# Weight read-backs issued by GpSimd instead of SyncE

## The chip, the core and the metric

One core of a Trainium2 chip runs the whole program. The metric is the time of one execution on the device in microseconds (us), as the median of several runs. The engines are named as the profile names them: PE (TensorE matmuls), PEld (TensorE weight loads), DVE (VectorE), ACT (ScalarE), POOL (GpSimd), SP (SyncE, which here does nothing but issue DMAs; SPq is its queue).

## What is computed

One layer of an encoder is applied to two inputs, a prompt of 1024 rows ("p") and a sample of 512 rows ("s"), with the same weights and a model width of 2048. All data are 32-bit floats.

```
h    = rmsnorm(x, pre_g)
proj = h @ w_in                       # 2048 x 5984, kept as 47 strips of 128 columns
q, k, v, gates, c_q, c_kv, k_pe, z    = parts of proj
o_a  = gated delta rule over q, k, v  # 8 heads, two directions, chunked scan
o_b  = softmax attention from c_q, c_kv (w_uq, w_uk, w_uv) and a rotary key, 8 heads
mix  = [o_a * silu(z_a), o_b * silu(z_b)]
y    = x + rmsnorm(mix @ w_out, post_g)
```

## The kernel before

Every large product is done in three passes. A weight tile is split into a high part `whi` and a rest `wlo`, each of 128 x 512 floats (256 KB), and the operand likewise into `hi` and `lo`; PE adds hi*whi, lo*whi and hi*wlo. `whi` and `wlo` together are called a piece here. A piece serves four k-tiles of 128.

The prompt goes through the input projection first (0 to about 1070 us). There a piece is loaded raw, ACT makes `whi` and POOL makes `wlo` (`split`, L199), and both are stored to DRAM (`spill`, L231). Later stages read the stored parts back instead of splitting again. There are two places that do so, L220 and L254:

- `kept_piece` (L220) for the input projection of the sample, 47 strips of 4 pieces of 2 reads, 376 reads, about 1070 to 1870 us. Beside it PE runs the delta rule (the `gdn_` functions).
- `read_back` (L254) for `mla_prep` (12 pieces for each of 3 blocks of 512 rows, 72 reads, about 1870 to 2070 us), for `attention` (32 reads), and for the first block of the output projection (`out_proj` with `more` set: 64 pieces, 128 reads, from about 2500 to 2867 us).

That makes 608 reads of 256 KB. A read waits until PE has finished with the buffer that it fills; there are four buffers of `whi` and of `wlo` in the projections and in `mla_prep` (`self.wb`, `read_back(..., 4)`), so up to three pieces can be on their way or ready ahead of the one in use.

All DMAs of the program are issued by SP, in one queue and in order: x and weight loads, read-backs, stores of results between the stages, the loads of the delta rule (`KQ`, `vp`, `ktok`, `dd`, `lam`, `lt`) and the swaps of `rope` (L567, L568). PE's order is written out by the program's own planner (`merge`, with a running time `self.t`); the order on the other engines is set by a scheduler from its own estimate of when each instruction can start.

POOL's work in the stages with read-backs: the running sum of squares of the sample (L313, 15 additions), clearing of two columns of `cin` (L349, L350), clearing of diagonal blocks (L776, which waits for the `dU` store), sums of squares (L381, L393), the sine product of `rope` (L570, which waits for the four or two swap DMAs), the softmax factors in `attention` (L1085, 160 times), and in the output projection the gain (L1219) and, from the second block on, the splits of `w_out` (L199).

Inside `out_proj` the first block is cut in parts: columns f = 0, 1, 2 over the first eight pieces, f = 3 over all sixteen, then f = 0, 1, 2 over the last eight. At the end of each of these last three, POOL runs L1219 four times.

Of the kernel before, what the change touches and what calls it, by code (L numbers as in the profile page):

```python
# [7 lines left out]
F32 = mybir.dt.float32  # L8
# [49 lines left out]
class Kern:  # L58
# [153 lines left out]
    def kept_piece(self, q, f, kt, lo_eng):  # L212

        nc, S = self.nc, self.scratch
        names = [f"w{v}{f}.{kt}" for v in "hl"]
        if q == "s":
            w = []
            for name, tag in zip(names, ("whi", "wlo")):
                t = self.wp.tile([P, 4, P], F32R, tag=tag, name=tag, bufs=self.wb)
                nc.sync.dma_start(t.bitcast(F32), S[name])  # L220
                w.append(t)
            return w
        return self.spill(names, self.a["w_in"][f][:, kt:kt + 4, :], lo_eng)
# [25 lines left out]
    def read_back(self, name, p, sfx, bufs):  # L249

        w = []
        for v, tag in zip("hl", ("whi", "wlo")):
            t = p.tile([P, 4, P], F32R, tag=tag + sfx, name=tag, bufs=bufs)
            self.nc.sync.dma_start(t.bitcast(F32), self.scratch[name + v])  # L254
            w.append(t)
        return w

# [1189 lines left out]
```

## Time and profile before

| | us |
|---|---|
| median of 3 runs | 3249.65 (3247.64 to 3258.47) |
| profiled execution, its own time | 3257.81 |
| its span in the trace | 3256.0 |
| PE busy | 3130.6 |
| DVE busy | 1643.3 |
| POOL busy | 885.1 |

The profiled execution's own time is 1.8 us more than the span that its trace covers. Busy times are sums over the span; issuing a DMA does not count as busy. The trace's granted clock of PE is 0.94 to 1.00 of full speed in every stage. Times within the span are counted from its start.

### The profile page before, as it was taken

What the parts mean: (1) busy time and instruction counts of PE and PEld (TensorE: products, weight loads), DVE (VectorE), ACT (ScalarE), POOL (GpSimd) and SP (SyncE); (2) the same over time, 40 slices, a digit from 0 to 9 for tenths busy, and PEclk for the clock granted to TensorE, in tenths of its full rate; (3) what the DMA queues carried; (4) which work ended last, traced back from release to release, by engine and by line L of the source; (5) the groups of instructions that cost most, each with busy time, mean ns of one, the idle gap of its engine ahead of it and who ended that gap; (6) DMA issues with size and microseconds to landing.
All of it is one profiled execution on the core that took longest, in us unless ns stands there. A gap on an engine that the chain in (4) does not pass through costs nothing.

```text
span 3256.0 us, 47971 instructions
## 1 busy us (share of the span) xinstructions
PE 3130.6 (96%) x16554; PEld 2611.5 (80%) x16554; DVE 1643.3 (50%) x4000; ACT 1159.2 (36%) x2736; POOL 885.1 (27%) x806
## 2 busy tenths in 40 slices
PE   7999999999999899999999988899999999899998
PEld 6788888888888788888888877688788878777876
DVE  7233443444410536765665477688887555240213
ACT  4223333333321313333333232465666444232231
POOL 5434434444432300000000011122222212044452
PEclk9999999999999999999999999999999999999999
DMA  6777777777776765566655697433223353764454
GB/s 242 248 229 236 241 242 242 240 233 244 242 244 203 256 197 181 182 193 198 212 177 179 215 302 250 151 97 90 67 89 119 101 188 117 247 217 126 149 175 133
DMA packets 405620, 626.10 MB, mean 192 GB/s; under 512 B 90544, under 2 KB 141736, under 8 KB 403840
## 3 DMA queue, kind: packets, MB, share of 16 engines
q1 hardware_dynamic: 405376, 623.04, 59.8%
q8 instruction: 130, 2.13, 0.3%
q14 instruction: 114, 0.93, 0.1%
HBM read 388.44 MB, written 230.90 MB: 190 GB/s over the span
## 4 chain that ended last, share of the span: by engine, by line
PE 74%; DMA 10%; DVE 8%; issue 3%; ACT 2%; POOL 2%; SPq 2%; DVEq 0%; POOLq 0%; ACTq 0%
PE mm L272 15%; PE mm L276 15%; PE mm L273 15%; PE py L1205 3%; PE py L1204 3%; PE py L1206 3%; DMA wraw<-w_out 2%; PE pt L1124 2%; PE Tp L841 2%; POOL wlo L199 1%; DVE UA L736 1%; PE py L904 1%; PE pu L923 1%; PE po L1102 1%; PE po L1101 1%
## 5 line engine op out<-in xcount | busy, mean ns | idle before, releaser
L272 PE MATMUL mm<-hi,whi 128*128 128x512 f32 x2256 | 899.6, 402 | 14.4 <-ACT whi L196 8.4
L273 PE MATMUL mm<-lo,whi 128*128 128x512 f32 x2256 | 877.4, 391 | 6.5 <-DVE lo L305 6.3
L199 POOL TENSOR_TENSOR wlo<-wraw,whi 128x512 fp32r<-128x512 f32 x400 | 561.2, 1412 | 750.5 <-ACT whi L196 610.6
L276 PE MATMUL mm<-hi,wlo 128*128 128x512 f32 x2256 | 763.8, 391 | 0.0
L196 ACT ACTIVATE whi<-wraw 128x512 fp32r<-128x512 f32 x400 | 248.6, 630 | 863.2 <-PE mm L273 314.1
L272 PEld LDWEIGHTS mm<-hi,whi 128*128 128x128 f32 x2256 | 425.6, 189 | 99.4 <-ACT whi L196 9.1
L273 PEld LDWEIGHTS mm<-lo,whi 128*128 128x128 f32 x2256 | 425.3, 189 | 90.9 <-DVE lo L305 9.4
L276 PEld LDWEIGHTS mm<-hi,wlo 128*128 128x128 f32 x2256 | 424.6, 188 | 91.0 <-DMA wlo<-wl43.4_8663 0.2
L1204 PE MATMUL py<-whi,mhi 128*128 128x512 f32 x768 | 303.4, 395 | 10.8 <-DVE y L1219 6.9
L1205 PE MATMUL py<-wlo,mhi 128*128 128x512 f32 x768 | 303.8, 396 | 6.8 <-POOL wlo L199 6.4
L1206 PE MATMUL py<-whi,mlo 128*128 128x512 f32 x768 | 302.4, 394 | 0.0
L1085 POOL TENSOR_TENSOR pe<-pe,af 128x512 f32<-128x512 f32 x160 | 166.2, 1056 | 491.1 <-DVE af L1083 202.7
L356 DVE SCALAR_TENSOR_TENSOR acc<-cin,conv_w,acc 128x1024 f32<-128x1024 f32 (+1 forms) x192 | 209.7, 1092 | 36.4 <-ACT acc L354 31.8
L352 DVE TENSOR_TENSOR cin<-mm,rbh 128x512 f32<-128x512 f32 x72 | 47.4, 687 | 302.5 <-PE mm L276 263.1
L1204 PEld LDWEIGHTS py<-whi,mhi 128*128 128x128 f32 x768 | 144.8, 189 | 45.9 <-DVE y L1219 8.0
L1205 PEld LDWEIGHTS py<-wlo,mhi 128*128 128x128 f32 x768 | 144.8, 189 | 43.7 <-POOL wlo L199 11.5
L1206 PEld LDWEIGHTS py<-whi,mlo 128*128 128x128 f32 x768 | 144.8, 189 | 31.9
L1071 ACT ACTIVATE pe<-s,am 128x512 f32<-128x512 f32 x160 | 110.3, 690 | 107.2 <-DVE am L1070 98.6
L1219 DVE TENSOR_TENSOR y<-py,g 128x512 f32<-128x512 f32 x36 | 24.7, 690 | 239.0 <-ACT junk L1218 235.5
L360 DVE TENSOR_TENSOR acc<-mm,rbh 128x512 f32<-128x512 f32 x48 | 31.7, 687 | 223.7 <-PE mm L276 212.5
L199 DVE TENSOR_TENSOR ptl<-pt,pth 128x512 fp32r<-128x512 f32 x160 | 109.8, 686 | 46.8 <-ACT pth L196 45.9
L1070 DVE TENSOR_REDUCE am<-s 128x1 f32<-128x512 f32 x160 | 109.5, 685 | 35.2 <-PE s L1067 34.6
(449 smaller groups left out, 5035.2 us busy)
## 6 DMA issues: line engine op xcount, KB each, us to landing
wraw<-w_out SPq DMA_DIRECT2D x192, 256.0 KB
wraw<-w_in SPq DMA_DIRECT2D x188, 256.0 KB
dd<-dX SPq DMA_DIRECT2D x48, 256.0 KB
x<-xT_p SPq DMA_DIRECT2D x16, 512.0 KB
xres<-x_p SPq DMA_DIRECT2D x8, 1024.0 KB
y_p<-y SPq DMA_DIRECT2D x32, 256.0 KB
x<-xT_s SPq DMA_DIRECT2D x16, 256.0 KB
xres<-x_s SPq DMA_DIRECT2D x4, 1024.0 KB
```

What stands on the lines that cost most here:

```text
L196: nc.scalar.activation(hi, src, AF.Copy)
L199: (lo_eng or nc.vector).tensor_sub(lo, src, hi.bitcast(F32))
L272: nc.tensor.matmul(ps, whi[:, k], hi[:, s], start=kt == 0, stop=False)
L273: nc.tensor.matmul(ps, whi[:, k], lo[:, s], start=False, stop=False)
L276: nc.tensor.matmul(ps, wlo[:, k], hi[:, s], start=False, stop=kt == KT - 1)
L356: nc.vector.scalar_tensor_tensor(acc, cin[:, j:j + T], w[:, f, j:j + 1], acc, op0=ALU.mult, op1=ALU.add)
L1070: nc.vector.tensor_reduce(m[:, k:k + 1], o, axis=AX.X, op=ALU.min)
L1071: nc.scalar.activation(pe[k], o, AF.Exp, bias=m[:, k:k + 1], scale=-1.0, accum_out=l[:, k:k + 1])
L1085: nc.gpsimd.tensor_mul(pe[k2], pe[k2], f[:, k2:k2 + 1].to_broadcast([P, BLK]))
L1204: nc.tensor.matmul(ps, hi[:, c], w[0], start=kt == kts[0], stop=False)
L1205: nc.tensor.matmul(ps, hi[:, c], w[1], start=False, stop=False)
L1206: nc.tensor.matmul(ps, lo[:, c], w[0], start=False, stop=kt == kts[1] - 1)
```

## The change

Both read-backs are issued by GpSimd. Nothing else is edited.

```diff
             for name, tag in zip(names, ("whi", "wlo")):
                 t = self.wp.tile([P, 4, P], F32R, tag=tag, name=tag, bufs=self.wb)
-                nc.sync.dma_start(t.bitcast(F32), S[name])
+                nc.gpsimd.dma_start(t.bitcast(F32), S[name])
                 w.append(t)
...
             t = p.tile([P, 4, P], F32R, tag=tag + sfx, name=tag, bufs=bufs)
-            self.nc.sync.dma_start(t.bitcast(F32), self.scratch[name + v])
+            self.nc.gpsimd.dma_start(t.bitcast(F32), self.scratch[name + v])
             w.append(t)
```

The scheduler places the reads among POOL's other instructions, so that SP's queue loses 608 entries and POOL's gains them. PE's order is the same but for a few rows in the attention stage. Three places follow, each with POOL's rows before and now. `wh33.4` is the high part of strip 33 from k-tile 4 on, `uq4h` the high part of strip 4 of w_uq, `o11.1l` the rest of k-tile 11 and column block 1 of w_out.

POOL at the start of the sample's input projection, before:

```order
L313 TENSOR_TENSOR rbh<-rbh,x 128x512
L637 MEMSET dd_9081 128x512
L313 TENSOR_TENSOR rbh<-rbh,x 128x512 x12
L349 MEMSET cin 128x2
L350 MEMSET cin 128x2
L313 TENSOR_TENSOR rbh<-rbh,x 128x512 x2
```

And now, around the last additions:

```order
L313 TENSOR_TENSOR rbh<-rbh,x 128x512 x5
L220 DMA whi<-wh33.0_746 128x512
L220 DMA wlo<-wl33.0_748 128x512
L220 DMA whi<-wh33.4_780 128x512
L220 DMA wlo<-wl33.4_782 128x512
L349 MEMSET cin 128x2
L350 MEMSET cin 128x2
L313 TENSOR_TENSOR rbh<-rbh,x 128x512 x3
```

The last three additions stand behind four reads.

POOL in `mla_prep`, before:

```order
L776 MEMSET UA 32x16x32 x4
L570 TENSOR_TENSOR rxs<-rxs,sin 128x512
L570 TENSOR_TENSOR rxs<-rxs,sin 64x512
L570 TENSOR_TENSOR rxs<-rxs,sin 128x512 x4
L570 TENSOR_TENSOR rxs<-rxs,sin 64x512
L570 TENSOR_TENSOR rxs<-rxs,sin 128x512 x2
```

And now:

```order
L776 MEMSET UA 32x16x32 x3
L254 DMA whi<-uq2h 128x512
L254 DMA wlo<-uq2l 128x512
L570 TENSOR_TENSOR rxs<-rxs,sin 128x512
L254 DMA whi<-uq3h 128x512
L254 DMA wlo<-uq3l 128x512
L254 DMA whi<-uq10h 128x512
L254 DMA wlo<-uq10l 128x512
L570 TENSOR_TENSOR rxs<-rxs,sin 64x512
L254 DMA whi<-uq4h 128x512
L254 DMA wlo<-uq4l 128x512
L254 DMA whi<-uq5h 128x512
```

Two to six reads stand between one sine product and the next.

POOL in the second half of the output projection's first block, before:

```order
L1219 TENSOR_TENSOR y_26029<-y_26029,g 128x512
L1219 TENSOR_TENSOR y_26030<-y_26030,g 128x512
L1219 TENSOR_TENSOR y_26031<-y_26031,g 128x512
L1219 TENSOR_TENSOR y_26032<-y_26032,g 128x512
L1219 TENSOR_TENSOR y_26029<-y_26029,g 128x512
```

And now, at the change from column block 0 to column block 1:

```order
L254 DMA wlo<-o10.1l 128x512
L254 DMA whi<-o10.1h 128x512
L1219 TENSOR_TENSOR y_26029<-y_26029,g 128x512
L254 DMA wlo<-o11.1l 128x512
L254 DMA whi<-o11.1h 128x512
L1219 TENSOR_TENSOR y_26030<-y_26030,g 128x512
L1219 TENSOR_TENSOR y_26031<-y_26031,g 128x512
L1219 TENSOR_TENSOR y_26032<-y_26032,g 128x512
L254 DMA wlo<-o12.1l 128x512
L254 DMA whi<-o12.1h 128x512
```

The reads of pieces 11 and 12 of the new column block stand behind gain products of the old one.

## Rows read from the trace of the kernel before

**Rows 1.** The page: busy time and share by engine; then the chain.

```profile
PE 3130.6 (96%) x16554; PEld 2611.5 (80%) x16554; DVE 1643.3 (50%) x4000; ACT 1159.2 (36%) x2736; POOL 885.1 (27%) x806
...
PE 74%; DMA 10%; DVE 8%; issue 3%; ACT 2%; POOL 2%; SPq 2%; DVEq 0%; POOLq 0%; ACTq 0%
```

**Rows 2.** Stretches by stage: start to end, length, busy us and instructions by engine.

```profile
core 0: us, PE busy (x) PEld busy (x) DVE busy (x) ACT busy (x) POOL busy (x), PEclk, DMA share, GB/s
1070.00:1122.00 52.00, 42.89 (x183) 33.54 (x181) 28.48 (x55) 18.82 (x39) 23.04 (x24) 0.94 0.90 318
1122.00:1870.00 748.00, 742.17 (x4320) 626.77 (x4321) 437.78 (x1418) 240.89 (x711) 30.15 (x83) 0.99 0.61 192
1870.00:2070.00 200.00, 175.03 (x1038) 144.09 (x1037) 141.03 (x382) 61.28 (x191) 28.29 (x23) 0.99 0.83 267
...
2500.00:2780.00 280.00, 266.58 (x1496) 224.98 (x1495) 153.00 (x333) 126.67 (x293) 63.60 (x61) 0.99 0.47 150
2780.00:2890.00 110.00, 100.98 (x431) 81.27 (x430) 40.48 (x61) 34.12 (x70) 25.45 (x19) 0.97 0.70 228
```

**Rows 3.** Waits of SP's queue, whole span: us in total, times, longest.

```profile
SPq L220 <- PE mm L276: 357.1, 152, 8.7
...
SPq L254 <- PE py L1206: 66.2, 36, 5.7
...
SPq L254 <- PE pq L610: 14.5, 8, 6.5
```

**Rows 4.** Line 254: one read's issue on SP (ns, min/median/max), and who waited.

```profile
L254 SPq DMA_DIRECT2D whi<-uq8h x3: 383/433/435, 1872.3 to 1983.4; - x3
...
  PE pq L608: 3.5, 1
  PE kp L1014: 2.2, 1
```

**Rows 5.** Waits of PE, 1870 to 2070 us.

```profile
PE kk L731 <- DVE z L969: 4.6, 1, 4.6
PE pk L882 <- DVE oacc L938: 4.6, 6, 1.2
PE py L904 <- DVE oacc L894: 4.4, 4, 1.9
```

**Rows 6.** Waits of DVE in the same stretch.

```profile
DVE rx L569 <- DMA rxs<-rx: 9.6, 4, 3.7
```

**Rows 7.** POOL groups, 1870 to 2070 and 2780 to 2890: busy, mean ns | idle before.

```profile
L570 POOL TENSOR_TENSOR rxs<-rxs,sin 128x512 f32<-128x512 f32 (+1 forms) x15 | 24.1, 1610 | 151.9 <-DMA rxs<-rx 112.6 <-DMA rxs<-kpe 24.1 <-DVE clo L591 10.0
...
L1219 POOL TENSOR_TENSOR y<-y,g 128x512 f32<-128x512 f32 x12 | 16.6, 1405 | 90.7 <-ACT junk L1218 90.7
```

**Rows 8.** The page's groups: the softmax factors on POOL.

```profile
L1085 POOL TENSOR_TENSOR pe<-pe,af 128x512 f32<-128x512 f32 x160 | 166.2, 1056 | 491.1 <-DVE af L1083 202.7
```

**Rows 9.** Waits of PE, 1070 to 1122, then 2070 to 2780 us.

```profile
PE xcols L325 <- POOL rbh L313: 0.7, 1, 0.7
...
PE pt L1124 <- POOL pe L1085: 1.4, 3, 1.0
```

**Rows 10.** PE in time, 2786 to 2787 us: two products three matmuls apart.

```profile
2786.25 0.39 PE L1206 MATMUL py<-whi,mlo 128*128 128x512 f32 x1
...
2786.93 0.39 PE L1206 MATMUL py<-whi,mlo 128*128 128x512 f32 x1
```

**Rows 11.** POOL in time, 1870 to 2070 us: start, length, [idle before it].

```profile
1894.54 1.29 POOL L570 TENSOR_TENSOR rxs<-rxs,sin 128x512 f32<-128x512 f32 x1 [20.22 <-DMA rxs<-rx]
...
1956.22 1.79 POOL L570 TENSOR_TENSOR rxs<-rxs,sin 128x512 f32<-128x512 f32 x1 [18.59 <-DMA rxs<-rx]
...
2016.08 1.29 POOL L570 TENSOR_TENSOR rxs<-rxs,sin 128x512 f32<-128x512 f32 x1 [15.38 <-DMA rxs<-rx]
```

**Rows 12.** Tile pq, 1870 to 2070 us: ns min/median/max, first and last start.

```profile
L608 PE MATMUL pq<-chi,whi x144: 389/398/988, 1875.3 to 2056.0; 128*128 128x512 f32 x144
```

**Rows 13.** The chain, 1910 to 1920 us: a read's time from issue to landing.

```profile
1912.76 5.53 DMA whi<-uq11h
```

## The prediction

> **What bounds the kernel now.** I read the page's busy line and chain first. PE is busy 3130.6 of 3256.0 us, and 74% of the chain that ended last is PE [rows 1]. All that any change off PE can win is therefore in PE's idle time, 125 us, and the stages with read-backs hold only part of that. The table of stretches says which part [rows 2]: the start of the sample's projection has 9.1 us of idle PE (52.0 - 42.9), its long body 5.8 (748.0 - 742.2), `mla_prep` 25.0 (200.0 - 175.0), the attention from 2500 on 13.4, the rest of the first output block 9.0.
>
> The reads do hold up SP's queue: SP stood 357.1 us before a read of line 220 and 66.2 + 14.5 us before one of line 254, always until PE had freed a buffer [rows 3]. All that is behind such a read in the queue waits with it. But almost nobody waits for the reads: the two largest waits for a read of line 254 are 3.5 and 2.2 us, both at the first read of a stage [rows 4]. So what counts is whether something else in SP's queue was late because of the reads, and where PE felt it. In the body of the projection PE is 99% busy, so there it was not felt. In `mla_prep` it may have been: DMA is busy 0.83 of the time [rows 2], and PE's largest waits are for DVE, 4.6 + 4.6 + 4.4 us [rows 5], while DVE in turn stood 9.6 us for the swaps of `rope` [rows 6], which go through SP.
>
> **The change, part by part.** It removes 608 issues from SP and puts 608 on POOL, each with its wait for PE. The bytes and the buffers are the same. On POOL everything behind a waiting read now waits too.
>
> The price of one issue on POOL is what the trace doesn't show, since every DMA of it is SP's. From below the nearest row is SP's own issue of the same read, 0.43 us [rows 4]; from above it is POOL's dearest instruction over 128 x 512 elements in these stages, the sine product with 1.61 us [rows 7]. I take 1.1 us, near the product of L1085 with 1.06 us [rows 8], because both are one pass of the engine's programs over 128 rows. It may fall outside; I keep 2 us for the range.
>
> *Body of the projection.* Some 350 of the 376 reads fall here, the others in the start. POOL has 30.2 us of work in 748 [rows 2]; 350 x 1.1 = 385 us more fit, and 350 x 1.61 = 564 us still do. POOL becomes the limit only at (748 - 30)/350 = 2.05 us. The gain can be no more than the 5.8 us of idle PE. I take -2.
>
> *Start.* POOL has 23.0 us of work in 52 and gets 24 reads: 23.0 + 24 x 1.1 = 49.4 us, which just fits; at 1.61 it is 61.6, 9.6 too many. The last three additions of L313 now stand behind four reads, and PE waits for the last of them already (0.7 us, [rows 9]). On the other side the x loads and the first `KQ` no longer share the queue with the reads. Between -4 and +9.6 I take 0.
>
> *`mla_prep`.* SP loses 72 x 0.43 = 31 us of issuing and 14.5 us of waiting for PE [rows 3, 4]. POOL has 28.3 us of work and gets 72 x 1.1 = 79, in 200: it fits. The swaps, the `dU` and `dX` transfers and the loads of the delta rule are issued sooner, DVE stands less for them, and the delta rule's products come less late. The gain lies between 0 and the 25 us of idle PE; I take half of the 13.6 us that PE waited for DVE [rows 5], -7.
>
> *Attention.* 32 reads and about 80 of w_out come between the softmax factors of L1085. A read that waits for PE's products of w_out now holds up the factors behind it; on SP these waits were 66.2 us in 36 times, 1.8 us each [rows 3]. PE waited only 1.4 us for the factors in all [rows 9], and they are made several steps ahead of their use, so most of it is covered. Without that cover some third of the 66.2 us would show, +20. I take +1.
>
> *First output block.* From 2797 on PE does 24 pieces back to back. Three matmuls take 0.68 us [rows 10], a piece of twelve 2.72, eight pieces 21.8 us. POOL needs for eight pieces 16 issues and, at the end of a column block, four gain products of 1.405 us [rows 7]: 16 x 1.1 + 5.6 = 23.2 us, 1.4 more than PE. And pieces 11 and 12 of the next block stand behind gain products of the old one, which costs a buffer's slack. Two such changes of block have reads behind them: 2 x 1.4, and 1 more for the order, +4.
>
> The sum is -2 + 0 - 7 + 1 + 4 = -4 us. Made against the profiled execution's own time, 3257.8 us, it gives 3253.8. That execution was 8.2 us above the median of the runs, 3249.65, so against the median I forecast **3246 us**, -0.1%. A measurement of this kernel can tell about 0.3%, 9.7 us, from no change, so this is "the same".
>
> The Trainium skill has a price for such a DMA: "SBUF — State Buffer", section "A bandwidth-pool intuition that's wrong (but worth ruling out)", says that one issued by GpSimd takes about 620 ns alone and 3100 ns beside a VectorE copy that locks the port both engines share. No run here shows either. By 0.62 us the output block would need 16 x 0.62 + 5.6 = 15.5 us for each 21.8, its term would be 0 and the time an estimated 3242 us; by 3.1 us the whole kernel would wait for POOL.
>
> **The rivals.**
>
> *POOL's issue sets the pace of the output block* (slower). The price decides: at a change of block POOL falls behind PE from (21.8 - 5.6)/16 = 1.01 us per issue, elsewhere in it from 21.8/16 = 1.36 us. At 1.61 us, 48 issues and eight gain products need 77.3 + 11.2 = 88.5 us against 65.3 of PE, +23, and the start adds its 9.6. In place of my +4 and 0 that is 3246 + 29 = **3275**. At 2 us the block alone is +42. For it: POOL's programs take 1.06 to 1.61 us over 128 rows in every group [rows 7, 8]. Against: making a list of transfers is not passing over 512 elements a row.
>
> *POOL's own waits hold up the reads* (slower, with any price). In `mla_prep` POOL stood 20.2, 18.6 and 15.4 us before single sine products, until the swaps had landed [rows 11]. Reads now stand behind these products. PE takes 36 pieces in 181 us [rows 12], 5.0 us each; three pieces ahead give 15 us, less 5.5 for a read to land [rows 13], so a hold of more than 9.5 us reaches PE: 10.7 + 9.1 + 5.9 = 26 us at most, about 13 if half of each hold passes while the reads ahead of it are issued. Then `mla_prep` gives +13 in place of -7: **3266**. Against it: the swaps are no longer behind reads in SP's queue, so the holds shrink.
>
> *SP's queue was the cause of more* (faster). If nearly all of PE's idle time in `mla_prep` comes from transfers that SP issued late, -7 becomes -18, and if the loads of the attention gain from the 66.2 us that SP no longer waits, another -5: **3230**.
>
> *The transfers themselves set the pace* (no change). In `mla_prep` the DMA engines are busy 0.83 of the time and a read takes 5.5 us to land against 0.43 us of issuing [rows 2, 4, 13]. If the swaps were late because of the transfers in front of them and not because of the queue, the -7 is 0, and with the -2 gone as well the time is 3246 + 9 = **3255**. The Trainium skill speaks for this one, in "DMA: Bandwidth & Descriptors", section "Issuing engines are not separate DMA queues": DMAs from all engines run on the same 16 DMA engines, and issuing from another only saves the sequencer's time. The trace agrees so far as 0.83 goes.
>
> **How the numbers follow.** My forecast gets 0.40, the pace of the transfers 0.10, POOL's issue 0.22, POOL's waits 0.10, the larger gain 0.18. By the bound of 9.7 us the forecast and the transfers are the same (0.50), the two POOL cases slower (0.32), the larger gain faster (0.18). The range takes in all rivals' times and the 2 us price of POOL's issue in part: 3230 to 3283. Below it lies a gain in several stages at once, above it an issue of 2 us and more that also reaches the body of the projection.
>
> **What would show it.** In the trace after, POOL's queue must show an issue's length near 1.1 us; under 1.0 the output block keeps its 110 us, above 1.4 PE waits there for `whi` and `wlo`. The stretch from 1122 to 1870 must stay within 10 us of its length. `mla_prep` should lose some 7 us, with DVE's 9.6 us for the swaps and PE's waits for DVE down. If PE waits for reads in `mla_prep` and POOL stands before L570 at that time, the second rival holds. SP's waits of lines 220 and 254 must be gone. The forecast is wrong if an issue on POOL costs far more than its other instructions do, or if the order on DVE, which the scheduler made anew, matters more than the queue.

## The result: 50 us slower

| | before | after |
|---|---|---|
| median (fastest to slowest), us | 3252.9 (3247.64 to 3258.47) | 3302.55 (3299.4 to 3307.69) |
| span of the profiled execution, us | 3256.0 | 3302.4 |

The ratio is 1.0155, with a 95% interval of 1.0137 to 1.0173: +50 us, where 3246 was predicted and 3283 was the upper end. The two spans differ by 46.4 us, and the rest of this text divides up that difference.

The page of the kernel after: busy time by engine, then the two DMA queues (packets, MB, share of 16 engines' span).

```profile
PE 3149.9 (95%) x16554; PEld 2626.5 (80%) x16554; DVE 1653.8 (50%) x4000; ACT 1159.6 (35%) x2736; POOL 1210.5 (37%) x1414
...
q1 hardware_dynamic: 317824, 463.61, 44.0%
q0 software_dynamic: 48640, 159.42, 15.0%
```

The 608 reads (608 x 0.2622 MB = 159.4) now travel in a queue of their own, q0. PE is busy 19.3 us longer than in [rows 1] with the same 16554 matmuls; the other 27.1 us are new idle time.

To see where, I cut both programs at the same matmuls, the first stage at a fixed 1040 us (cut at a matmul there, the starts of the kernels below come out up to 2.0 us shorter or 1.6 longer). The stretches of the kernel after (start to end, length, busy us and instructions by engine, granted clock, DMA share, GB/s):

```profile
core 0: us, PE busy (x) PEld busy (x) DVE busy (x) ACT busy (x) POOL busy (x), PEclk, DMA share, GB/s
1040.00:1172.40 132.40, 115.09 (x480) 91.12 (x479) 62.00 (x152) 33.17 (x64) 57.36 (x79) 0.91 0.65 215
1172.40:1885.80 713.40, 703.43 (x4147) 594.37 (x4146) 415.54 (x1319) 231.09 (x692) 203.53 (x409) 1.00 0.59 189
1885.80:2097.10 211.30, 182.83 (x1040) 151.53 (x1038) 140.39 (x387) 61.98 (x191) 67.22 (x96) 0.94 0.79 251
...
2529.70:2934.10 404.40, 372.07 (x1925) 310.71 (x1924) 195.16 (x392) 161.28 (x363) 165.02 (x223) 0.96 0.51 166
```

| stage | before, us | after, us | change | of it PE idle | of it PE busy |
|---|---|---|---|---|---|
| start of the sample's projection | 120.0 (from 1040) | 132.4 | +12.4 | +7.6 | +4.8 |
| its body, with the delta rule | 708.0 | 713.4 | +5.4 | +4.8 | +0.6 |
| `mla_prep` | 198.0 | 211.3 | +13.3 | +5.7 | +7.6 |
| attention | 434.0 | 432.6 | -1.4 | -1.4 | 0 |
| first output block | 390.0 | 404.4 | +14.4 | +9.9 | +4.5 |
| rest | 366.0 | 368.3 | +2.3 | +2.4 | -0.1 |

Up to 1040 us, where there are no reads, the length is the same (1.9 us less idle, 1.9 more busy). Two executions of one order of work can differ by some 5 us in a stage (two kernels below with the same order have 5.2 and 9.8 us in `mla_prep`), so only the larger entries mean something one by one. In the body the execution before is a long one: the kernels below whose reads of L220 and loads of L771 stay on SP have 702.7 to 706.6 us there, one of them with its very order up to 2400 us.

### The profile page after: what moved, and what is told of

Read it like the earlier page. It is cut to its first block, busy times and chain, and to the rows that moved or that the text cites. A ratio compares the mean times of both kernels' runs of the same rounds, so it can differ in the third digit from the quotient of the medians.

```text
span 3302.4 us, 48042 instructions
## 1 busy us (share of the span) xinstructions
PE 3149.9 (95%) x16554; PEld 2626.5 (80%) x16554; DVE 1653.8 (50%) x4000; ACT 1159.6 (35%) x2736; POOL 1210.5 (37%) x1414
## 4 chain that ended last, share of the span: by engine, by line
PE 35%; DMA 10%; DVE 8%; issue 2%; ACT 2%; POOL 1%; SPq 1%; POOLq 0%; DVEq 0%; ACTq 0%
PE mm L272 3%; PE mm L276 3%; PE mm L273 3%; PE py L1204 3%; PE py L1205 3%; PE py L1206 3%; DMA wraw<-w_out 2%; PE pt L1124 2%; POOL wlo L199 1%; PE Tp L841 1%; DVE XT L789 1%; PE py L904 1%; DVE tm L787 1%; PE po L1102 1%; PE kk L731 1%
## 5 line engine op out<-in xcount | busy, mean ns | idle before, releaser
L196 ACT ACTIVATE whi<-wraw 128x512 fp32r<-128x512 f32 x400 | 248.8, 630 | 864.2 <-PE mm L273 319.5
L1205 PEld LDWEIGHTS py<-wlo,mhi 128*128 128x128 f32 x768 | 145.5, 190 | 45.5 <-POOL wlo L199 13.8
L1219 DVE TENSOR_TENSOR y<-py,g 128x512 f32<-128x512 f32 x36 | 24.7, 690 | 239.9 <-ACT junk L1218 236.8
L199 DVE TENSOR_TENSOR ptl<-pt,pth 128x512 fp32r<-128x512 f32 x160 | 110.0, 687 | 47.2 <-ACT pth L196 46.2
```

The lines of the kernel that those rows point to most:

```text
L196: nc.scalar.activation(hi, src, AF.Copy)
L199: (lo_eng or nc.vector).tensor_sub(lo, src, hi.bitcast(F32))
L1205: nc.tensor.matmul(ps, hi[:, c], w[1], start=False, stop=False)
```

## The experiments

Two things changed at once: the queue of the reads, and the order of the other instructions, which the scheduler made anew. By the traces (line and tile) 640 of DVE's 4000 instructions stand elsewhere, 128 of ACT's 2736, and 191 of the 1948 other DMAs in SP's own queue. The first two experiments set them apart. In them the program is built once with the reads on one engine, the order of each engine is noted, and in a second build, with the reads on the other engine, that order is imposed. The added dependencies set the order of issue on one engine alone and add no wait (in the first trace PE, DVE, ACT and SP's other DMAs stand exactly as before):

```diff
+        keep = DependencyInfo(NoSync, DATA)
+        for e in (PE, DVE, Activation, SP, Pool):
+            names = [n for n in plan[e] if n in traced and engine_of(traced[n]) == e]
+            for first, then in zip(names, names[1:]):
+                tc.add_manual_dep(traced[then], first, keep, reason="order")
```

**The queue alone** (the order of before, all 608 reads on GpSimd).

> All 608 reads are issued by GpSimd, but every other instruction of PE, DVE, ACT, SP and POOL keeps the place that it has in the kernel before (edges that fix the order of issue and add no wait). Theory ORDER: the loss of 50 us comes from the order that the scheduler made anew on DVE, ACT, SP and POOL, and issuing from GpSimd costs next to nothing; then this kernel takes 3245 to 3262 us, as before. Theory QUEUE: the loss comes from GpSimd issuing the reads (its 0.54 us each, its waits in order, what it does to DVE beside it); then it takes 3285 to 3310 us, as after.

Measured 3304.77 us, ratio 1.0159 (1.0137 to 1.0182): the queue by itself costs what the whole change costs.

**The order alone** (the order of after, the reads on SP).

> The opposite: all reads stay on SyncE, but every other instruction of PE, DVE, ACT, SP and POOL stands where it stands in the changed kernel. ORDER: the loss comes with the order, 3285 to 3310 us. QUEUE: nothing is issued by GpSimd, so it takes 3245 to 3262 us. A time between the two in both kernels would mean that each has a share.

Measured 3283.11, ratio 1.0085 (1.0057 to 1.0113), +31 us. So the order costs too, and the two don't add up (53 + 31 against 50): either one uses up much of the slack that the other would.

**One place alone.** Only L220 is edited, then only L254.

> Only the 376 reads of line 220 (input projection of the sample) are issued by GpSimd, the 232 of line 254 stay on SyncE; the scheduler orders everything anew. PE's lag behind the kernel before was 17 us at the end of the projection in the changed kernel. If each stage's loss belongs to its own reads: 3253 + 17 = 3270 us, and the lag after the projection does not grow. ORDER allows any time from 3240 to 3300, since a new order reaches stages whose reads were not touched; QUEUE wants the 17 us inside the projection alone.

> Only the 232 reads of line 254 (mla_prep, attention, first output block) are issued by GpSimd. If each stage's loss belongs to its own reads: 3253 + 29 = 3282 us, with no lag before 1870 us and 15 us of it in mla_prep (from 17 to 32 in the changed kernel). ORDER allows 3240 to 3300 with lags that do not follow the reads.

Measured 3283.69 (1.0089, 1.0063 to 1.0114) and 3280.9 (1.0085, 1.0061 to 1.0109). The second is as expected, the first lost 32 us where 17 were expected. Each loses where its reads are: L220 +10.1 at the start and +14.3 in the body, L254 +14.8 in `mla_prep` and +13.8 in the output block. So the losses are local, though both kernels have orders of their own, which may have part in them.

**The start.** POOL's queue in the kernel after (start, length, engine, line, [idle before it and what ended it]):

```profile
1095.70 0.56 POOL L220 DMA_DIRECT2D whi<-wh46.8_360  x1 [6.16 <-PE mm L276]
...
1097.86 1.30 POOL L313 TENSOR_TENSOR rbh<-rbh,x 128x512 f32<-128x512 f32 x1
```

An addition of L313 has to wait while the reads ahead of it wait for PE to free a buffer. L313 is the last reader of an x tile, and the next x goes into its buffer, so SP's load of the next x (L297) waits for it. SP's waits from 1062 to 1130 us, kernel after (waiting line <- what ended it: us in total, times, longest):

```profile
SPq L297 <- POOL rbh L313: 10.4, 5, 4.1
```

Before it was 3.2 us in three times, in the first experiment 12.3 in seven. Behind the x loads in SP's queue stand the delta rule's first loads (`KQ`). PE's waits from 1040 us to the end of the start, first experiment (queue alone), then the kernel after:

```profile
...
PE kk L731 <- DMA KQ<-f9p: 3.0, 1, 3.0
PE xcols L325 <- POOL rbh L313: 1.3, 1, 1.3
PE mm L272 <- DMA whi<-wh32.8_370: 0.6, 1, 0.6
```

```profile
PE abps L489 <- DVE cacc L373: 6.1, 1, 6.1
PE mm L272 <- DVE acc L360: 5.7, 1, 5.7
```

By the queue alone it is many small pieces, each a little longer than before (before: `KQ` 1.8, L313 0.7, the read none), and PE's busy time in this stage is 4.2 us longer (114.49 against 110.29). In the full change the two largest are due to the order: with the order alone they are 4.6 and 7.5 us, with the queue alone 0.2 and 4.0 (before 0.2 and 3.4). `KQ` is not waited for there.

**The body: a round trip through DRAM.** Once in each turn the delta rule stores `dU` (L764, SP), loads it back in two other shapes (`lam` and `lt`, L771, SP), and copies parts of `lt` into `lam` (L779, ACT). In the kernel before all of this and the reads stood in one queue. SP's queue at one turn, before:

```profile
1870.25 1.93 SPq L764 DMA_DIRECT2D dUp<-UA  x4
1872.28 0.43 SPq L254 DMA_DIRECT2D whi<-uq8h  x1
...
1875.76 0.60 SPq L771 DMA_DIRECT2D lt<-dUp  x1
1877.03 0.43 SPq L254 DMA_DIRECT2D wlo<-uq0l  x1
```

Three reads go out (the first is shown), then the four loads of L771, then the next reads. The same turn after, on POOL and then on SP; POOL issues eight reads between the first and the last line:

```profile
1889.63 0.54 POOL L254 DMA_DIRECT2D whi<-uq8h  x1 [10.53 <-DVE acc L360]
...
1893.85 0.54 POOL L254 DMA_DIRECT2D wlo<-uq9l  x1
...
1891.69 0.55 SPq L771 DMA_DIRECT2D lam<-dUp  x1
...
1893.90 0.63 SPq L771 DMA_DIRECT2D lt<-dUp  x1
```

And ACT's copies that wait for `lt`, before and then after:

```profile
1878.00 2.24 ACT L779 COPY lam<-lt 64x256 f32<-64x256 f32 x4 [3.95 <-DMA lt<-dUp]
```

```profile
1900.55 1.14 ACT L779 COPY lam<-lt 64x256 f32<-64x256 f32 x2 [5.54 <-DMA lt<-dUp]
1904.42 1.14 ACT L779 COPY lam<-lt 64x256 f32<-64x256 f32 x2 [2.73 <-DMA lt<-dUp]
1905.59 0.47 ACT L936 COPY oacc<-pu 128x128 f32<-128x128 f32 x2
```

From the end of the last L771 issue to the first copy it was 1878.00 - 1876.36 = 1.6 us; now it is 1900.55 - 1894.53 = 6.0, and the second half comes 3.9 us later still. Summed over the first eight turns this is 9.6 us before, 20.8 after, 18.8 in the first experiment, 11.1 with the order alone. In the attention stage these four kernels have 0.7 to 1.2 us a turn. In the body PE waits almost only for work that stands on ACT behind these copies: in the kernel before and in the first experiment each of its waits over 0.7 us ends within 2.3 us of the last copy's end. Its longest waits there, before and then in the first experiment:

```profile
PE crow L450 <- ACT acc L471: 2.8, 1, 2.8
PE pu L920 <- ACT yb L913: 1.2, 1, 1.2
```

```profile
PE crow L450 <- ACT acc L471: 4.6, 1, 4.6
PE pu L920 <- ACT yb L913: 2.6, 2, 2.3
PE py L904 <- ACT oacc L897: 1.9, 1, 1.9
```

All its waits for ACT there add up to 5.1 us before, 11.8 in the first experiment, 9.4 after and 2.6 with the order alone. My second theory was that the two queues share the transfers, so that reads beside the trip make it late, and that the common queue had kept them out of its way. Two kernels test it. The first is the queue-alone kernel with the 48 loads of L771 moved to GpSimd as well, where reads and loads keep the order that they had on SP. The second leaves the reads on SP and moves those 48 loads alone.

```diff
-                nc.sync.dma_start(t[d * 64:d * 64 + 64],
+                nc.gpsimd.dma_start(t[d * 64:d * 64 + 64],
```

> As e1 (reads issued by GpSimd, all other work in the old order), but the 48 small loads of the delta rule, lam and lt (line 771), are issued by GpSimd too, in the order in which they stood among the reads on SyncE: one queue again, only another engine's. New theory TRIP: in the old queue no read could travel while SyncE stood before these loads for the dU store, and the next reads went out behind them; from a queue of their own the reads travel at the same time, lt lands 1 to 2 us later, ACT stands at the copies of line 779 (27.1 us in all before, 45.4 in e1, 51.7 in the changed kernel) with the scan's work behind them, and PE idles and then runs at half clock. TRIP expects 3250 to 3270 us and ACT's wait for lt at 25 to 33 us. If anything else about GpSimd's queue costs the time (its 0.54 us an issue, its waits in order, late reads), it stays at 3295 to 3310.

> The mirror image: all reads stay on SyncE, only the 48 loads of lam and lt (line 771) are issued by GpSimd; all other work in the old order. TRIP: reads and loads are in two queues again, so ACT's wait for lt is 38 to 55 us and the time 3275 to 3305 us, though GpSimd issues only 48 transfers and no read. If the loss belongs to reads that GpSimd issues: 3250 to 3262.

Measured 3295.12 (1.0119, 1.0096 to 1.0142) and 3271.36 (1.0043, 1.0029 to 1.0057). By its total the one-queue kernel failed the theory: 3250 to 3270 was expected, and 3295 stands at the edge of what I had set for the case that something else about GpSimd's queue costs the time. ACT's waits for `lt` fell only from 45.4 to 40.3 us, where 25 to 33 were expected. The second total lies between its two ranges. Only the body agrees. Its stretch in the queue-alone kernel and, second, with one queue again:

```profile
1168.00:1889.90 721.90, 708.45 (x4147) 598.01 (x4146) 413.79 (x1319) 231.31 (x692) 203.56 (x409) 0.99 0.58 187
```

```profile
1169.70:1880.40 710.70, 703.18 (x4147) 593.30 (x4146) 413.32 (x1319) 231.08 (x692) 215.52 (x433) 1.00 0.59 190
```

721.9 us become 710.7, against 708.0 before, although POOL issues more. The trips' sum falls from 18.8 to 13.0, and PE's waits for ACT from 11.8 to 5.6 us. With the loads alone in the other queue the body has +8.5, the trips 21.8 and PE's waits for ACT 11.1, without one read on POOL. (Part of that may be that GpSimd's small loads come late by themselves: 1.1 to 3.0 us in the attention stage of these two kernels, where SP's take 0.7 to 1.2. But the one-queue kernel loads by GpSimd too and has 13.0.) So two queues cost time in the body, and the trip accounts for some 10 of the 53 us.

**Must it be ACT?** ACT stands at L779 with the scan's work behind it, and in the kernel after its waits for `lt` are 46.2 + 5.5 us, against 27.1 before. I moved the copies to DVE, with the reads on SP and then on GpSimd in that same order.

```diff
-                nc.scalar.copy(lam[i][64:, :, 16 * k:16 * k + 16],
+                nc.vector.tensor_copy(lam[i][64:, :, 16 * k:16 * k + 16],
```

> The kernel before with the copies of line 779 on DVE instead of ACT, reads on SyncE; the scheduler orders anew. It is the base for e8. ACT no longer stands for lt; DVE stands there anyway before line 787. TRIP expects 3235 to 3265 us (a new order alone moved the time by up to 31 us in e2).

> e7 with all 608 reads issued by GpSimd and everything else in e7's order, so that only the queue differs between the two. If ACT standing at line 779 is the road by which late loads reach PE, e8 is at most 25 us above e7 (DVE still stands for lt). If the loss has another road, e8 is again some 50 us above e7, as e1 is above the kernel before.

Measured 3258.25 (1.0007, 0.9994 to 1.002) and 3313.05 (1.0166, 1.0142 to 1.019). The queue costs 55 us here too, where at most 25 were expected if ACT's standing were the road: the body goes from -4.7 to +12.5, the trips from 11.6 to 22.8. So who copies `lt` makes no difference; whoever does stands for it. For the rest of the 55 us this shows no cause.

**Start and body together.** The one-queue kernel still lost +9.7 at the start. Here the 24 reads of the first three strips go back to SP (the edit shown), and only turns 1 to 8 load by GpSimd; 584 reads stay on GpSimd.

```diff
-                nc.gpsimd.dma_start(t.bitcast(F32), S[name])
+                (nc.sync if f in (46, 32, 33) else nc.gpsimd).dma_start(t.bitcast(F32), S[name])
```

> As e5 (reads and the loads of lam and lt in one queue on GpSimd, the rest in the old order), with two edits: the first three strips of the sample (46, 32, 33; 24 reads, the start of the projection) are read from SyncE again, and only turns 1 to 8 of the delta rule, which fall beside reads, load lam and lt from GpSimd. 584 of the 608 reads stay on GpSimd. Theory HOLD for the start: GpSimd stood 20 us there for PE before reads, its additions of line 313 stood behind them, the x buffers that these additions free came late, and SyncE's x loads waited 12 to 16 us for them instead of 3.2. Then the start (1040 to 1160 us) loses 0 to 2 us in place of 8 to 10, the attention 0 in place of 5, and the time is 3295 - 8 - 5 = 3282, between 3270 and 3285 us. If the start's loss has another cause than these reads, the time is 3288 to 3296.

Measured 3280.63, ratio 1.0086 (1.0068 to 1.0103), as expected. Its start and its body:

```profile
1040.00:1160.20 120.20, 111.47 (x475) 89.15 (x474) 56.47 (x152) 32.49 (x63) 42.82 (x54) 0.94 0.69 235
...
1160.20:1869.80 709.60, 702.68 (x4147) 593.52 (x4146) 413.15 (x1319) 230.98 (x692) 215.53 (x433) 1.00 0.59 190
```

The start is back at +0.2 (+1.8 if cut at a matmul; SP's waits for L313: 2.9 us in two times), the body at +1.6. The queue-alone kernel, which differs in the start by these 24 reads alone, had +8.0 there. What is left, +7.5 in `mla_prep`, +5.2 in the output block, +6.2 behind it, I could not assign.

**Where the new order costs.** With the reads on SP, the order of after is imposed only up to about 2400 us, and then only from there on (by the trace 39 instructions on DVE and 45 on ACT stand elsewhere).

> All reads on SyncE. The first part of the program, up to the middle of the attention (about 2400 us), stands in the order of the changed kernel, the rest in the old one. If what the new order costs is lost at a few places, each by itself, this kernel has e2's losses up to there and none after: +10 at the start, -5 in the projection, +5 in mla_prep, together +10 on 3254: 3258 to 3270 us. If the order costs time only through the whole chain, e10 and e11 do not add up to e2's 31 us.

> The other half: all reads on SyncE, the old order up to about 2400 us, the changed kernel's order after it (53 rows of DVE and 46 of ACT differ). Expected by places: +11 in the output block of the prompt (a first row of line 1218 on ACT and of line 1219 on DVE stands behind one more split that waits for a load) and 0 to +6 after it: 3262 to 3274 us.

Measured 3271.99 (1.0057, 1.0042 to 1.0072) and 3267.03 (1.0045, 1.0031 to 1.0058): +20 and +15, in sum about the +31 of the whole, the first 2 us above what I expected. The early part loses at the start (+10.4) and in `mla_prep` (+9.8), the late part in the first output block, +12.9. PE's waits in that block, kernel after, then with the late order and the reads on SP:

```profile
PE py L1204 <- DVE y L1219: 8.9, 1, 8.9
PE s L1063 <- ACT kh L196: 6.9, 1, 6.9
PE py L1204 <- DVE y L1215: 6.0, 1, 6.0
...
PE pt L1124 <- DVE al L1081: 3.7, 1, 3.7
```

```profile
PE py L1204 <- DMA mraw<-mix13p: 7.8, 1, 7.8
PE pt L1124 <- DVE al L1081: 7.5, 1, 7.5
PE s L1063 <- ACT kh L196: 7.0, 1, 7.0
PE py L1204 <- DVE y L1215: 4.8, 1, 4.8
```

In the kernel before, `kh` L196 is waited for 0.7 us, `y` L1215 1.9, and `al` is not among the waits; `y` L1219 has 6.9 us in two times, so its 8.9 is only 2.0 more. The largest new wait is the one for `kh`. ACT at that place, before and then after:

```profile
2620.47 0.60 ACT L196 ACTIVATE kh<-kp 128x512 fp32r<-128x512 f32 x1 [0.65 <-PE kp L1016]
```

```profile
2653.32 0.63 ACT L196 ACTIVATE mhi<-mraw 128x512 fp32r<-128x512 f32 x1 [3.92 <-DMA mraw<-mix10p]
...
2657.55 0.63 ACT L196 ACTIVATE mhi<-mraw 128x512 fp32r<-128x512 f32 x1 [1.72 <-DMA mraw<-mix11p]
...
2660.21 0.58 ACT L196 ACTIVATE kh<-kp 128x512 fp32r<-128x512 f32 x1
```

In the new order three splits of `mraw` stand before the split of `kh`, and two of them wait for their loads. For the wait of 8.9 us a moved row can be seen too; ACT's order, before (`-`) and after (`+`):

```
 L196 ACTIVATE mhi_29744<-mraw 128x512
+L196 ACTIVATE mhi_29750<-mraw 128x512
 L1218 ACTIVATE junk,ss<-py_28507 128x512
-L196 ACTIVATE mhi_29750<-mraw 128x512
 L1218 ACTIVATE junk,ss<-py_28508 128x512
```

The last rows of one column block's norm (L1218) now stand behind a split that waits for a load. ACT after, with PE's wait ending at 2843.86:

```profile
2841.85 0.63 ACT L196 ACTIVATE mhi<-mraw 128x512 fp32r<-128x512 f32 x1 [0.80 <-DMA mraw<-mix12p]
2842.39 0.58 ACT L1218 ACTIVATE junk<-py 128x512 f32<-128x512 f32 x1
```

That such rows cost these waits is read from the timelines, and was not tried by itself.

**A version to beat both?** If `lt` is so costly, its copies might go to GpSimd, which has least to do (order of before, reads on SP).

> The kernel before, reads on SyncE and everything in the old order, but the copies of line 779 run on GpSimd instead of ACT: what does it cost the kernel before that ACT stands for lt (27.1 us in 14 times)? GpSimd has 30 us of work in 748 there and stands for nobody. If ACT's stand reaches PE as the trip theory says, some 5 to 10 us of PE's waits behind ACT go and the time is 3238 to 3250 us, faster than both kernels; if GpSimd's slower copies and DVE's own wait for lam take the place of it, it is 3250 to 3262.

Measured 3262.41, ratio 1.0027 (1.0016 to 1.0039). It is slower: DVE now waits 35.6 us for these copies. No version here beats the kernel before.

## Why the prediction was wrong

**The start, "I take 0".** This step failed, by 12. The place was seen ("the last three additions of L313 now stand behind four reads"), but priced by PE's wait for the last sum alone, [rows 9], which hardly grew. Two things were put at nothing. One is that L313 also frees the x buffers, so that SP's loads stand behind POOL: in the order of before, reads on GpSimd cost +8.0 here, and +0.2 with the 24 first ones back on SP. The other is the new order, which by itself costs +10 in this stage without any read on POOL; PE's largest waits in the full change are the order's (`cacc` 6.1, `acc` 5.7). Which moved rows make these two late stays open.

**The body, "I take -2".** This step failed, by 7 (by 16 where the old order is kept). It priced issuing and found that POOL has room, which it has. It did not ask what the common queue did for the others: it kept the order of the transfers. The kernels with one queue have +2.7 and +1.6 in the body, and those with two have +14 and +8.5 in the order of before and +14.3 and +12.5 in two others. The full change has only +5.4, but the order alone has -4.6 (703.4 us) there, so in its own order the queue added 10.1.

**`mla_prep`, -7.** The sign failed. The mechanism was there: DVE's waits for the swaps, 9.6 us in [rows 6], fell, and so did POOL's 151.9 us before L570 in [rows 7] (there POOL now stands before reads instead, 77.1 us for `pq` L610). DVE's waits in 1885.8 to 2097.1 us, kernel after, then POOL's group:

```profile
DVE rx L569 <- DMA rxs<-rx: 6.1, 4, 2.7
...
L570 POOL TENSOR_TENSOR rxs<-rxs,sin 128x512 f32<-128x512 f32 (+1 forms) x15 | 24.5, 1633 | 42.1 <-DMA rxs<-rx 24.7 <-DMA rxs<-kpe 5.2 <-DMA q6p<-rx 5.1
```

But DVE stood there 11.3 us for `lam` (5.6 before), and PE waited 5.03 us for a row that ACT did behind the late copies (L936, shown above; 0.8 before). The step assumed that SP's other transfers can only gain when the reads leave; by these rows, those that the reads had stood behind lost more. The trip is not all of it: with one queue `mla_prep` still has +4.8 and +7.5, and the new order alone has +5.2 and +9.8. What each cost in the full change stays open.

**The first output block, +4.** The size fits the queue alone (+4.3), but by luck, and the main term was missing. POOL issues there at half the price assumed, and in the kernel after PE waits for reads 0.8 us at most. The +14.4 is the new order, given by it alone (+11.4, +12.9). The last sentence of the prediction named the scheduler's order as a danger and gave it no price; it should have been a rival with a bound, since every engine's rows could be compared.

**The issue on POOL, 1.1 us.** Too high. Line 254's reads on POOL (ns, min/median/max, first and last start):

```profile
L254 POOL DMA_DIRECT2D whi<-uq8h x3: 538/538/579, 1889.6 to 2010.4; - x3
```

The longest of all, the first read, is 709 ns, so the rival that POOL's pace sets the end fell, though its 3275 is nearer the result than the forecast.

**POOL's own waits.** The second rival was right in kind, with the roles reversed: not POOL's work held reads, but waiting reads held POOL's work, and at the start. **The transfers set the pace** was right that the transfers are shared, and wrong in "no change". The Trainium skill, "DMA: Bandwidth & Descriptors", section "Issuing engines are not separate DMA queues", says that DMAs of all engines interleave and that another issuer only saves the sequencer's time. The trips here agree with the first half; the second half, read as "it can do no harm", is contradicted by +53 us in the queue-alone kernel. **SP's queue as cause of more** fell: its waits of L220 and L254 are gone, and no stage gained more than 1.4 us.

**Only PE's idle time was counted.** All terms were made of PE's idle time, but 19.3 of the 46.4 us are longer busy time for the same matmuls. PE after, at the start of a stretch that follows idle time, then windows (granted clock behind ACT's and POOL's columns), the first of them from the kernel before at the same place, where PE had been idle 3.43 us:

```profile
1087.71 0.80 PE L272 MATMUL mm<-hi,whi 128*128 128x512 f32 x1 [5.67 <-DVE acc L360]
...
1093.42 0.59 PE L273 MATMUL mm<-lo,whi 128*128 128x512 f32 x1
1093.84 0.40 PE L276 MATMUL mm<-hi,wlo 128*128 128x512 f32 x1
```

```profile
1085.80:1088.50 2.70, 2.66 (x6) 2.15 (x7) 1.59 (x1) 2.33 (x4) 2.54 (x3) 0.50 0.97 330
...
1087.70:1093.80 6.10, 6.09 (x14) 4.79 (x15) 3.47 (x4) 2.29 (x4) 1.76 (x2) 0.50 1.03 355
...
1905.90:1909.60 3.70, 3.69 (x13) 3.29 (x14) 3.32 (x15) 1.76 (x5) 0.00 (x0) 0.54 0.82 255
```

After 5.67 us of idle PE 14 matmuls run at the level of 1.2 GHz (0.50), one each 0.43 us where later ones come each 0.23. So this idle time cost another 14 x 0.20 = 2.8 us. The kernel before paid 6 x 0.20 = 1.2 of them too, so 1.6 are new, of the +4.8 of busy time in this stage. The last row shows the same after the 5.03 us that PE waited for ACT in `mla_prep`. That all of the 19.3 us come about in this way was not counted up stretch by stretch.

**Right:** the attention (next to nothing, +1 against -1.4), SP's waits for reads gone, and POOL having room for the issues.

## What to carry to other kernels

Before a transfer is moved to another queue, ask which small loads stood behind or ahead of it in the old one. Here the shared queue had also kept bulk reads away from a round trip that engines wait for, and on the new engine the additions behind waiting reads were late, with the loads into the buffers that they free. With both put right, 584 reads on GpSimd still cost 28 us, and no run here says why. Where a scheduler orders the other engines, build both programs and price the rows that moved; here that alone was worth 31 us. Count for each new idle stretch of PE what follows it at half the clock.

## What was unexpected of the hardware

A 256 KB read is issued by GpSimd in 0.538 us (median of 608; 0.709 at most) against 0.38 on SP before (median; 0.32 to 1.85). Beside DVE it takes no longer: 414 of the 608 issues overlap a DVE instruction, and their median is that of the other 194. The one exception is the kernel with copies on DVE and reads on GpSimd: its only four later issues over 0.6 us (0.636 to 0.763) all run beside a copy of L779 or a scaling of L304 on DVE (others beside these lines take 0.54 to 0.55). The Trainium skill, "SBUF — State Buffer", section "A bandwidth-pool intuition that's wrong (but worth ruling out)", has about 620 ns alone and 3100 ns beside a port-locking VectorE copy; nothing near the second was seen here. The reads of L220 land 2.7 us at the least, 3.2 in the median and 8.4 at the most after the start of their issue, those of L254 2.7, 3.9 and 11.7.
